# A hybrid decoder layer on one NeuronCore: the first half written as a table of steps, k and q0 projected first, the softmax scaling moved from GpSimd to VectorE

## The chip, the cores and the metric

The kernel runs on one core of one Trainium2 chip. A core has a matrix engine (TensorE, PE in the rows), three further engines that compute (VectorE, ScalarE, GpSimd: DVE, ACT, POOL in the rows) and SyncE (SP), which issues most DMA transfers. Each engine takes its own instructions in order and waits for the others on semaphores. The metric is the time of one launch in microseconds.

## The reference

One decoder layer in fp32 on a sequence of 1024 tokens with 1024 channels:

```python
h = rms_norm(x, norm_mix_g)
q, k, v, u, gate = split(h @ w_in)          # 512, 128, 128, 512, 512 columns
q, k = rms_norm per head of 64              # 8 query heads, 2 kv heads
a = sliding_window_gqa(q, k, v, sinks, rel_bias)   # window 128, blocks of 128 queries
c = u * sigmoid(gate)
c = silu(layer_norm(causal_depthwise_conv31(c)))
mix = concat(rms_norm(a), rms_norm(c))
x = x + mix @ w_out
h = rms_norm(x, norm_mlp_g)
x = x + square(relu(h @ w_up)) @ w_down     # hidden 4096
```

In the attention each block of 128 queries sees its own and the previous block of keys, with a bias from a table and one sink value per head in the softmax.

## The kernel before

Activations lie with channels on the partitions. A product in fp32 is made of three matmuls on operands split into a high and a low part: hi·hi, hi·lo, lo·hi (`mm3k`, lines 194 to 200). A weight tile is 128 output channels by 1024 (8 blocks `kc`); with two halves h of 512 tokens it makes 48 matmuls of 128x512. These are called dense here. The low part of a weight tile (`wlo`, L168) is made on VectorE, the high part (`whi`, L167) on ScalarE, some tiles ahead of use.

The layer's first part has these stages:

- `start` loads x, makes its squares' sum for the RMS norm and multiplies the first two weight tiles while x arrives.
- The combined projection: pairs u0 to u3 (a u tile and its gate tile; `ug`, then `hglu` and `conv`), q0 to q3, k and v (`qkv`). `qk_stats` makes the norms of q and k heads, with a power on GpSimd (L507).
- 16 attention units (j, bp), head pair j and block pair bp. `attn_a`: QK on PE into two banks `sc` (L567), scaling on ScalarE (L574), bias and maximum on VectorE in one reduce (L575). `attn_b`: the maximum's arithmetic, four exps on ScalarE (L591), the sum `den` and its reciprocal on VectorE, and the scaling of the probabilities on GpSimd (L596, L597, L599). `attn_c`: transposes on PE (L616), their evacuation `pT`, PV on PE (L625), evacuation into Q.
- Conv: layer norm `ln` (token Z), `silu` (S), `norm_conv` (C); attention's norm `norm_attn` (N). C and N write the halves of `mix`, split into high (ScalarE, L658) and low (GpSimd, L659).
- Output projection in two parts: `out_conv(h)` with the conv's half of mix, `out(h)` with attention's half; `out` also sums squares of the result (L744 on GpSimd). `x1_norm` (X) and `gen_h0`, `gen_h1` (G) make the normalised, split input of the MLP.
- The MLP: ten first tiles of up (`up_first`), then `up` and `down`, which form sums of blocks so that fewer products are needed.

What comes in which order is set by a string of tokens: `d` is one step of the dense generator chain, `u` one unit (its `attn_a`, with `attn_b` of two units earlier and `attn_c` of four units earlier), letters with a half start a slow generator, `+n` advances it. Everything but the dense work is emitted at a raised priority; a scheduler then orders each engine's instructions from the emission, the priorities and the readiness that it expects.

```python
ORDER = "u1,u2,u3,k,q0,v,q1,q2,q3"
SCHED = "d d d d d d d d d d d d Z0 Z1 S0 S1 C0 C1 d +2 d +2 ..."
```

Of the kernel before, what the change touches and what calls it, by code (L numbers as in the profile page):

```python
# [12 lines left out]
F32 = mybir.dt.float32  # L13
# [20 lines left out]
NU1 = 2  # L34
# [3 lines left out]
BOOST0 = 3000  # L38
BOOST = 200
LAG_B = 2  # L40
LAG_C = 4
UNITS = "00,01,10,11,20,21,30,31,02,03,12,13,22,23,32,33"
ORDER = "u1,u2,u3,k,q0,v,q1,q2,q3"
SCHED = "d d d d d d d d d d d d Z0 Z1 S0 S1 C0 C1 d +2 d +2 d +2 d +2 d +4 d +4 u d +1 u d +1 u d +1 u d +1 u d +1 u d +1 u d d u d u d d u d u d u d N0 +9 u d u d u d u d u d u d u d u d X0 N1 G0 +2 d +2 d +2 d +2 d +2 d +2 d +2 d +2 d d d d d d d d d d d X1 G1 +1 d +3 d +2 d +2 d +2 d +2 d +2 d +2 d +2"
# [22 lines left out]

class Builder:
    def __init__(self, ctx, tc, io):
        self.tc = tc  # L70
        self.nc = tc.nc
        self.io = io
# [52 lines left out]

    def run(self, gen):
        for _ in gen:
            self.flush()

    def flush(self):  # L130
        while self.bg_step(1):
            pass

    def slow_step(self, n):
        for _ in range(n):
            while self.slow:
                with self.tc.high_priority(self.slow[0][1]) if self.slow[0][1] else ExitStack():
                    self.pin_all = self.slow[0][2]
                    more = next(self.slow[0][0], None) is not None
                    self.pin_all = False  # L140
                    if more:
                        break
                self.slow.pop(0)

    def bg_step(self, n):
        for _ in range(n):
            if not self.bg:
                return False
            with self.tc.high_priority(BOOST):
                if next(self.bg[0], None) is None:  # L150
                    self.bg.pop(0)
        return True
# [41 lines left out]
    def mm3k(self, ps, w, x, kc, first, last):  # L194
        nc = self.nc
        ws = slice(kc * P, (kc + 1) * P)
        xh, xl = x
        nc.tensor.matmul(ps, w[0][:, ws], xh, start=first, stop=False)  # L198
        nc.tensor.matmul(ps, w[0][:, ws], xl, start=False, stop=False)  # L199
        nc.tensor.matmul(ps, w[1][:, ws], xh, start=False, stop=last)  # L200
# [14 lines left out]
    def build(self):  # L215
# [29 lines left out]
        for _ in range(4):  # L245
            nc.tensor.matmul(ps[:, :256], zero[:, :P], zero[:, :256], start=True, stop=True)
# [15 lines left out]
        nc.scalar.activation(warm, self.mhalf[:, 0:1], AF.Sigmoid)  # L262
        self.conv_load(0)
        self.start()
        self.mix = {}
        self.bg = []
        self.slow = []
        self.rq_done = set()
        self.qkv_begin()
# [19 lines left out]
        for tok in SCHED.split():  # L289
# [8 lines left out]
            elif tok[-1] == "d":  # L298
                for _ in range(int(tok[:-1] or 1)):
                    next(dense)  # L300
                    self.flush()
# [10 lines left out]
        for _ in dense:  # L312
            pass
# [843 lines left out]
```

## Time and profile before

| | |
|---|---|
| time, median of 3 runs | 1023.99 us (1022.13 to 1025.24) |
| the profiled execution's own time | 1022.33 us |
| its span (first to last instruction) | 1020.4 us |
| mean granted clock of PE | 0.983 |
| PE busy | 996.5 us (98%) |
| VectorE busy | 668.7 us (66%) |
| ScalarE busy | 493.2 us (48%) |
| GpSimd busy | 104.1 us (10%) |

The profile is one execution. PE is busy for nearly the whole span, but matmuls in the first part sometimes run at a lower granted clock, which counts as busy as well. Averages over the span mix the stages, so the rows further below are cut into stretches. The ScalarE order holds seven loads of an activation table, the GpSimd order 86 rows.

### The profile page before, as it was taken

The numbers are of one execution on the slowest core, as the hardware profiler recorded it, in microseconds if no ns is written. First come the engines' busy times: TensorE is split into PE (matmuls) and PEld (weight loads), VectorE is DVE, ScalarE is ACT, GpSimd is POOL, SyncE is SP. The second block draws the span as 40 slices with busy tenths as digits, with TensorE's granted clock in tenths as the row PEclk, the third lists the DMA queues.
The fourth block names the chain that finished last, engine by engine and source line by source line (L and its number), as shares of the span: only waits on it lengthen the run. The fifth ranks groups of instructions, "written<-read, shape, count | busy, mean of one in ns | idle before, by whom it ended". The sixth has DMA issues, their size and how long they took to land.

```text
span 1020.4 us, 14870 instructions
## 1 busy us (share of the span) xinstructions
PE 996.5 (98%) x5560; PEld 806.2 (79%) x5560; DVE 668.7 (66%) x1150; ACT 493.2 (48%) x946; POOL 104.1 (10%) x82
## 2 busy tenths in 40 slices
PE   8999999899979989999999999999999999999998
PEld 7888887677657768778888888888888888888886
DVE  7456535266667484598777786777774777747763
ACT  7332325766757445475444544536454343443442
POOL 1000012255143322200000000000000000000000
PEclk9999999799979999999999999999999999999999
DMA  9123300002200234446556655667875532346451
GB/s 354 60 70 136 125 32 11 11 12 93 73 11 32 90 122 139 145 171 215 194 194 220 237 185 205 239 225 255 285 264 188 183 130 99 103 135 216 165 165 42
DMA packets 67464, 148.72 MB, mean 146 GB/s; under 512 B 7776, under 2 KB 8032, under 8 KB 66880
## 3 DMA queue, kind: packets, MB, share of 16 engines
q1 hardware_dynamic: 67248, 147.75, 42.3%
q8 instruction: 44, 0.72, 0.3%
q14 instruction: 28, 0.23, 0.1%
q10 hardware_dynamic: 144, 0.02, 0.0%
HBM read 106.98 MB, written 38.80 MB: 143 GB/s over the span
## 4 chain that ended last, share of the span: by engine, by line
PE 89%; DVE 5%; ACT 3%; issue 1%; DMA 1%; POOL 0%; DVEq 0%; SPq 0%; ACTq 0%
PE mm L198 7%; PE mm L199 7%; PE mm L200 7%; PE sc L837 4%; PE sc L839 4%; PE sc L838 4%; PE tr L839 3%; PE tr L837 3%; PE tr L838 3%; PE sc L567 3%; PE mm L839 3%; PE mm L837 3%; PE mm L838 3%; PE mm L1057 3%; PE mm L1058 3%; PE mm L1059 3%
## 5 line engine op out<-in xcount | busy, mean ns | idle before, releaser
L763 ACT CAST wb<-wd 128x512 fp32r<-128x512 f32 x80 | 49.8, 622 | 111.3 <-DVE wd L1025 41.7
L764 DVE TENSOR_TENSOR wb<-wd,wb 128x512 fp32r<-128x512 f32 x80 | 55.3, 691 | 69.9 <-ACT wb L763 69.9
L167 ACT CAST whi<-raw 128x512 fp32r<-128x512 f32 (+1 forms) x54 | 42.9, 795 | 77.2 <-PE mm L199 55.4
L198 PE MATMUL mm<-xh,whi 128*128 128x512 f32 x192 | 77.8, 405 | 0.0
L199 PE MATMUL mm<-xl,whi 128*128 128x512 f32 x192 | 77.2, 402 | 0.0
L200 PE MATMUL mm<-xh,wlo 128*128 128x512 f32 x192 | 77.2, 402 | 0.0
L764 DVE TENSOR_TENSOR wb<-hb,wb 128x512 fp32r<-128x512 f32 x112 | 76.8, 685 | 0.0
L837 PE MATMUL sc<-op,wb 128*128 128x512 f32 x192 | 74.7, 389 | 0.0
L838 PE MATMUL sc<-op,wb 128*128 128x512 f32 x192 | 74.7, 389 | 0.0
L839 PE MATMUL sc<-op,wb 128*128 128x512 f32 x192 | 74.7, 389 | 0.0
L763 ACT CAST wb<-hb 128x512 fp32r<-128x512 f32 x112 | 69.0, 616 | 0.3 <-PE sc L839 0.3
L168 DVE TENSOR_TENSOR wlo<-raw,whi 128x512 fp32r<-128x512 f32 (+1 forms) x54 | 52.8, 979 | 16.8 <-ACT whi L167 11.5
L763 ACT CAST wb<-raw 128x512 fp32r<-128x512 f32 x46 | 27.7, 621 | 65.4 <-DVE raw L891 33.0
L198 PE MATMUL mm<-mix,whi 128*128 128x512 f32 x128 | 52.6, 412 | 3.3 <-ACT x1g L763 2.9
L200 PE MATMUL mm<-mix,wlo 128*128 128x512 f32 x128 | 52.5, 410 | 0.3 <-DVE wlo L168 0.3
L199 PE MATMUL mm<-mix,whi 128*128 128x512 f32 x128 | 52.4, 410 | 0.0
L1058 PE MATMUL mm<-wb,wb 128*128 128x512 f32 x128 | 49.8, 389 | 0.0
L1058 PE MATMUL sc<-wb,wb 128*128 128x512 f32 x128 | 49.8, 389 | 0.0
L837 PE MATMUL tr<-op,wb 128*128 128x512 f32 x128 | 49.8, 389 | 0.0
L838 PE MATMUL tr<-op,wb 128*128 128x512 f32 x128 | 49.8, 389 | 0.0
L1059 PE MATMUL mm<-wb,wb 128*128 128x512 f32 x128 | 49.6, 389 | 0.0
L1059 PE MATMUL sc<-wb,wb 128*128 128x512 f32 x128 | 49.6, 389 | 0.0
(270 smaller groups left out, 2532.9 us busy)
## 6 DMA issues: line engine op xcount, KB each, us to landing
hb<-hid SPq DMA_DIRECT2D x112, 256.0 KB, 2.9
wd<-w_down SPq DMA_DIRECT2D x80, 256.0 KB, 4.4
raw<-w_up SPq DMA_DIRECT2D x27, 512.0 KB, 3.5
hid<-h SPq DMA_DIRECT2D x48, 256.0 KB, 2.9
pa<-pa SPq DMA_DIRECT2D x20, 512.0 KB, 4.5
raw<-w_out SPq DMA_DIRECT2D x32, 256.0 KB, 2.6
hid<-pa SPq DMA_DIRECT2D x32, 256.0 KB, 2.9
hid<-tu SPq DMA_DIRECT2D x32, 256.0 KB, 3.3
```

Source lines behind the costliest of these rows:

```text
L167: self.pin(nc.scalar.copy(hi, raw))
L168: self.pin(eng.tensor_tensor(lo, raw, hi.bitcast(F32), ALU.subtract))
L198: nc.tensor.matmul(ps, w[0][:, ws], xh, start=first, stop=False)
L199: nc.tensor.matmul(ps, w[0][:, ws], xl, start=False, stop=False)
L200: nc.tensor.matmul(ps, w[1][:, ws], xh, start=False, stop=last)
L763: self.pin(self.nc.scalar.copy(hi, src))
L764: self.pin(eng.tensor_tensor(lo, src, hi.bitcast(F32), ALU.subtract))
L837: nc.tensor.matmul(ps, wh[:, c], xh, start=first and k == 0, stop=False, skip_group_check=True)
L838: nc.tensor.matmul(ps, wh[:, c], xl, start=False, stop=False, skip_group_check=True)
L839: nc.tensor.matmul(ps, wl[:, c], xh, start=False, stop=last and k == len(xs) - 1, skip_group_check=True)
L1058: nc.tensor.matmul(pss[m], wh[:, c], bl, start=False, stop=False, skip_group_check=True)
L1059: nc.tensor.matmul(pss[m], wl[:, c], bh, start=False, stop=f == NP - 1, skip_group_check=True)
```

## The change

The token string, the priorities and the background generators are gone. A table `SIDE` says which pieces of side work are emitted at which of the numbered steps; a step is 12 dense matmuls, since `mm3` now yields in its middle. Units A (QK and softmax), T (transposes) and V (PV) are three pieces. `start` multiplies k and q0 instead of u0 and its gate. The dense order is u0 to u3, v, q1 to q3, both out_conv, both out, the ten up_first. Units of j = 0 stand beside u1 to u3, the other twelve at steps 43 to 57. `Pinned` sends each PE instruction through `put`, which keeps program order where `on` is True; the code sets `on` to False in both places where it sets it.

```diff
-ORDER = "u1,u2,u3,k,q0,v,q1,q2,q3"
-SCHED = "d d d d d d d d d d d d Z0 Z1 S0 S1 C0 C1 d +2 ..."
+ORDER = "u0,u1,u2,u3,v,q1,q2,q3"
+U_EARLY, U_LATE = (9, 13, 17, 21), ("10", "11", "20", "21", "30", "31", "12", "13", "22", "23", "32", "33")
+LATE = (43, 44, 47, 48, 51, 51, 52, 53, 54, 55, 56, 57)
+SIDE = {2: "rs", 3: "st4 st0", 5: "rb st0", 6: "st4", 7: "st4", 12: "c0", 20: "c1", 28: "c2",
+        36: "c3", 37: "vt", 38: "vt Z0", 40: "Z1", 41: "st1", 42: "st1 S0 S0", 43: "S0 S0", 44: "S1 S1", 45: "S1 S1",
+        46: "C0 st2", 47: "C0 C0 st2", 49: "st3 C1", 50: "st3", 51: "C1 C1",
...
+for n, at in enumerate(U_EARLY):
+    SIDE[at] = SIDE.get(at, "") + f" A0{n}"
+    SIDE[at + 4] = SIDE.get(at + 4, "") + f" T0{n}"
+    SIDE[39 + n] = SIDE.get(39 + n, "") + f" V0{n}"
...
+class Pinned:
+    def __init__(self, tc):
+        self.tc, self.on = tc, False
+
+    def put(self, ins):
+        if self.on:
+            self.tc.keep_in_program_order(ins)
...
     def mm3(self, ps, w, xs):
         for kc, x in enumerate(xs):
+            if kc == 4:
+                yield True
             self.mm3k(ps, w, x, kc, kc == 0, kc == len(xs) - 1)
...
+        k = 0
+        while True:
+            for a in SIDE.get(k, "").split():
+                if a[0] == "A":
+                    st[a[1:]] = self.attn_a(int(a[1]), int(a[2]))
+                    self.attn_b(st[a[1:]])
...
+            k += 1
+            if not next(dense, False):
+                break
...
-            ps = [self.psum("x"), self.psum("o")]
+            ps = [self.psum(t) for t in (("x", "o"), ("sc", "sc"))[jh]]
...
-        if bp == 0:
-            nc.gpsimd.tensor_tensor(s[:, 0:2, P:], s[:, 0:2, P:], rd[:, 0:2].unsqueeze(2).broadcast_to([P, 2, P]), ALU.mult)
-            nc.gpsimd.tensor_tensor(s[:, 2:4, :], s[:, 2:4, :], rd[:, 2:4].unsqueeze(2).broadcast_to([P, 2, 256]), ALU.mult)
-        else:
-            nc.gpsimd.tensor_tensor(s, s, rd.unsqueeze(2).broadcast_to([P, 4, 256]), ALU.mult)
+        for i in range(4):
+            lo = P if bp == 0 and i < 2 else 0
+            nc.vector.tensor_scalar(s[:, i, lo:], s[:, i, lo:], rd[:, i:i + 1], None, ALU.mult)
...
-            self.evac(EVAC.get(u["i"], "aaa")[c], pT[:, c, i0 * P:], ps[:, i0 * P:])
+            self.evac("a" if u["j"] == 0 else "v", pT[:, c, i0 * P:], ps[:, i0 * P:])
...
-            nc.gpsimd.tensor_tensor(mt[:, 1, :], s, mt[:, 0, :].bitcast(F32), ALU.subtract)
+            nc.vector.tensor_tensor(mt[:, 1, :], s, mt[:, 0, :].bitcast(F32), ALU.subtract)
...
+        rs = self.small("rs1", 4)
+        self.rsqrt(rs, mv3[:, :, 1], 1.0, 4)
...
-                nc.gpsimd.tensor_tensor(acc, acc, sq, ALU.add)
+                nc.vector.tensor_tensor(acc, acc, sq, ALU.add)
```

`ln` makes the powers of its four tiles in one instruction. Tiles of the output X for h = 1 and slots of the operand tiles `op` and `wd` lie in other pools. The order of the weights' loads follows the dense order.

How the change moves instructions is seen in the orders that the scheduler built. First GpSimd, between two of the norms' powers, from the middle of the first part: before, the softmax scalings of a unit (s by rd) and the low halves of mix stand between them.

```order
L507 TENSOR_TENSOR qst_2035<-qst_2035,mhalf 128x16
L599 TENSOR_TENSOR s_1982<-s_1982,rd_2147 128x1024
L596 TENSOR_TENSOR s_2085<-s_2085,rd_2261 128x2x128
L597 TENSOR_TENSOR s_2085<-s_2085,rd_2261 128x512
L210 TENSOR_TENSOR rc_2140<-rs_2141,mhalf 128x4
L599 TENSOR_TENSOR s_2181<-s_2181,rd_2356 128x1024
L659 TENSOR_TENSOR mix_2245<-y_498,mix_2245 128x512
```

In the change the whole of GpSimd's work after the start is powers: r for x, qst for q and k, rs for the layer norm, rc for the norms of mix and x1.

```order
L505 TENSOR_TENSOR qst_410<-qst_410,mhalf 128x16
L207 TENSOR_TENSOR rs_211_1838<-rs_1839,mhalf 128x4
L207 TENSOR_TENSOR rs_227_1917<-rs_1918,mhalf 128x4
L505 TENSOR_TENSOR qst_1965<-qst_1965,mhalf 128x16
L505 TENSOR_TENSOR qst_2201<-qst_2201,mhalf 128x16
L207 TENSOR_TENSOR rc_2234<-rs_2235,mhalf 128x4
L505 TENSOR_TENSOR qst_2394<-qst_2394,mhalf 128x16
L207 TENSOR_TENSOR rc_2481<-rs_2482,mhalf 128x4
```

So 86 rows became 30, and every 128x512 or larger operation has left GpSimd.

Second VectorE, in one of the late units, beside the output projection. Before, its queue has reduces (ISA is the custom reduce, with a read of its result), small operations of the maximum and of den, an evacuation, and a residual add and a low half for the weights:

```order
L575 ISA s_2561,mx_2562<-s_2561,bias_304 128x256
L575 ISA mx_2562 128x1
L727 TENSOR_TENSOR X_2670<-mm_2657,xr_2655 128x512
L593 TENSOR_TENSOR den_2602<-den_2602,es_2601 128x4
L603 COPY pT_2615<-tr_2616 128x256
L594 RECIPROCAL rd_2603<-den_2602 128x4
L168 TENSOR_TENSOR wlo_2728<-raw_2577,whi_2727 128x512
```

In the change the same piece of a unit reads:

```order
L588 TENSOR_TENSOR den_2697<-den_2697,es_2696 128x4
L581 SCALAR_TENSOR_TENSOR nm_2775<-mx_2760,nsink 128x4
L589 RECIPROCAL rd_2698<-den_2697 128x4
L582 TENSOR_TENSOR es_2776<-nm_2775,nsink 128x4
L720 TENSOR_TENSOR Xp_3093<-mm_3137,xr_3135 128x512
L592 TENSOR_SCALAR s_2679<-s_2679,rd_2698 128x256 x4
L596 COPY pT_2815<-tr_2816 128x512
L163 TENSOR_TENSOR wlo_3186<-raw_3072,whi_3185 128x512
L596 COPY pT_2815<-tr_2822 128x512
```

Four scalings and both evacuations of each late unit have come into VectorE's queue, ahead of the low half for a weight tile of the output projection.

Third ScalarE, at the layer norm's silu (L696 and L693; y from the transposed z). Before, the silus of the first half stand together, and a table load comes where the function changes:

```order
L592 ACT_TABLE_LOAD
L592 ACTIVATE es_1883<-es_1883 128x4
L574 ACTIVATE s_1815<-sc_1817,rq 128x256 x2
L574 ACTIVATE s_1815<-sc_1818,rq 128x256 x2
L696 ACT_TABLE_LOAD
L696 ACTIVATE y_498<-tr_1730,pv 128x512
L696 ACTIVATE y_787<-tr_1736,pv 128x512
```

In the change, rows 140 to 156 of ScalarE's order:

```order
L693 ACTIVATE y_1472<-tr_2030,pv 128x512
L693 ACTIVATE y_1748<-tr_2036,pv 128x512
L586 ACT_TABLE_LOAD
L586 ACTIVATE s_2042,den_2060<-s_2042,nm_2058 128x128 x2
L586 ACTIVATE s_2042,den_2060<-s_2042,nm_2058 128x256 x2
L587 ACTIVATE es_2059<-es_2059 128x4
L162 CAST whi_2137<-raw_1752 128x512
L484 COPY Q_307<-mm_2017 128x512
L693 ACT_TABLE_LOAD
L693 ACTIVATE y_767<-tr_2090,pv 128x512
L586 ACT_TABLE_LOAD
```

Units and silus alternate there; the whole order has eleven table loads where the one before has seven.

## Rows read from the trace of the kernel before

**Rows 1.** Windows: stretch, length; busy (count) PE, PEld, DVE, ACT, POOL; PEclk, DMA, GB/s

```profile
50.00:150.00 100.00, 100.00 (x1397) 81.37 (x1396) 52.19 (x58) 30.86 (x48) 2.90 (x1) 1.00 0.27 90
150.00:231.00 81.00, 75.46 (x393) 60.07 (x392) 42.31 (x126) 52.22 (x126) 30.19 (x25) 0.93 0.04 14
231.00:412.00 181.00, 172.00 (x909) 129.53 (x908) 111.77 (x243) 103.42 (x255) 62.18 (x41) 0.94 0.25 82
460.60:1016.20 555.60, 555.37 (x2448) 459.11 (x2447) 393.26 (x627) 248.59 (x434) 0.00 (x0) 1.00 0.55 188
200.00:350.00 150.00, 144.39 (x803) 105.62 (x803) 91.56 (x242) 96.91 (x273) 62.17 (x41) 0.92 0.15 46
290.00:305.00 15.00, 13.63 (x51) 9.51 (x52) 7.99 (x17) 6.93 (x20) 7.99 (x6) 0.61 0.01 1
365.00:385.00 20.00, 16.61 (x64) 12.79 (x64) 19.19 (x26) 8.82 (x14) 5.15 (x4) 0.91 0.40 132
```

**Rows 2.** Matmul lines: duration ns min/median/max, first and last start (us), form

```profile
L198 PE MATMUL mm<-xh,whi x192: 387/389/774, 28.5 to 226.1; 128*128 128x512 f32 x192
L198 PE MATMUL mm<-mix,whi x128: 387/390/628, 230.2 to 411.0; 128*128 128x512 f32 x128
L837 PE MATMUL mm<-x1g,wb x48: 389/389/389, 460.6 to 691.2; 128*128 128x512 f32 x48
```

**Rows 3.** Timeline 221.5 to 225: start us, us, engine, line, operation

```profile
221.87 2.10 DVE L575 CUSTOM_DVE_ANT_0 s<-s,bias 128x256 f32<-128x256 f32 x1
224.16 0.42 DVE L575 CUSTOM_DVE_ANT_0 s<-s,bias 128x256 f32<-128x256 f32 x1
...
221.80 1.89 POOL L599 TENSOR_TENSOR s<-s,rd 128x1024 f32<-128x1024 f32 x1 [1.25 <-DVE rd L594]
```

**Rows 4.** Lines by source: duration ns min/median/max, first and last start (us)

```profile
L575 DVE CUSTOM_DVE_ANT_0 s<-s,bias x64: 260/423/2109, 169.9 to 325.6; 128x256 f32<-128x256 f32 x56, 128x128 f32<-128x128 f32 x8
...
L168 DVE TENSOR_TENSOR wlo<-raw,whi x54: 659/693/2095, 20.6 to 454.2; 128x512 fp32r<-128x512 f32 x32, 128x1024 fp32r<-128x1024 f32 x22
...
L507 POOL TENSOR_TENSOR qst<-qst,mhalf x5: 2899/2904/3391, 130.3 to 243.4; 128x16 f32<-128x16 f32 x5
...
L210 POOL TENSOR_TENSOR rc<-rs,mhalf x6: 1007/1014/1969, 196.6 to 418.4; 128x4 f32<-128x4 f32 x6
```

**Rows 5.** VectorE's groups: busy us, mean ns; idle before, releaser

```profile
L575 DVE CUSTOM_DVE_ANT_0 s<-s,bias 128x256 f32<-128x256 f32 x56 | 37.8, 706 | 6.0 <-ACT s L574 5.8
L648 DVE SCALAR_TENSOR_TENSOR y<-y,pv,sc 128x512 f32<-128x512 f32 x8 | 5.4, 743 | 4.4 <-PE sc L393 4.4
L603 DVE COPY pT<-tr 128x512 f32<-128x512 f32 x5 | 3.4, 686 | 2.4 <-PE tr L616 2.4
L593 DVE TENSOR_TENSOR den<-den,es 128x4 f32<-128x4 f32 x16 | 2.6, 161 | 11.2 <-ACT es L592 9.4 <-ACT s L591 1.9
L603 DVE COPY Q<-o 128x256 f32<-128x256 f32 x6 | 2.5, 424 | 5.1 <-PE o L625 5.1
L518 DVE COPY kc<-rk 128x512 f32<-128x512 f32 x2 | 0.8, 424 | 0.0
```

**Rows 6.** PE's groups from 50 to 150 us

```profile
L198 PE MATMUL mm<-xh,whi 128*128 128x512 f32 x103 | 40.9, 397 | 0.0
```

**Rows 7.** Chain of work: start us, us, what

```profile
245.55 1.02 PE tr L616 x8
...
320.33 1.06 PE sc L567 x6
321.39 0.81 PE o L625 x12
```

**Rows 8.** ScalarE's groups: busy us, mean ns; idle before, releaser

```profile
L696 ACT ACTIVATE y<-tr,pv 128x512 f32<-128x512 f32 x8 | 5.8, 774 | 0.1
L696 ACT ACT_TABLE_LOAD x3 | 3.8, 1283 | 0.1
L637 ACT ACTIVATE sq<-y 128x512 f32<-128x512 f32 x6 | 3.8, 640 | 1.4 <-PE tr L501 1.4
```

More of the change, by code (lines that the diff above doesn't have):

```diff
@@ L124, in chain @@
                 yield True
[L126 to L152, printed above, removed]
     def load_w(self, src):
@@ L245, in build @@
         for _ in range(4):
-            nc.tensor.matmul(ps[:, :256], zero[:, :P], zero[:, :256], start=True, stop=True)
+            self.pe.matmul(ps[:, :256], zero[:, :P], zero[:, :256], start=True, stop=True)
         self.ones = cp.tile([P, 1], F32, tag="ones", name="ones")
@@ L262, in build @@
         nc.scalar.activation(warm, self.mhalf[:, 0:1], AF.Sigmoid)
+        self.mix = {}
+        self.gens = {}
+        self.hg = [None] * NCT
+        self.start()
         self.conv_load(0)
[L264 to L269, printed above, removed]
         self.X = {}
@@ L280, in build @@
-        dense.append(self.out(1))
-        dense += [self.up_first(i) for i in FIRST[NU1:]]
-        dense.append(self.up())
-        dense.append(self.down())
+        dense = [make[n]() for n in ORDER.split(",")]
+        dense += [self.out_conv(0, range(KC)), self.out_conv(1, range(KC)), self.out(0), self.out(1)]
+        dense += [self.up_first(i) for i in FIRST]
         dense = self.chain(dense)
-        units = [(int(a[0]), int(a[1])) for a in UNITS.split(",")]
+        side = {"Z": self.ln, "S": self.silu, "C": self.norm_conv, "N": self.norm_attn, "X": self.x1_norm,
+                "G": lambda h: self.gen_h0(h) if h == 0 else self.gen_h1(h)}
@@ L311, in build @@
-        assert i >= n + LAG_C
-        for _ in dense:
-            pass
+        k = 0
[4 more added lines that the diff above has]
+                    self.attn_b(st[a[1:]])
+                elif a[0] == "T":
+                    self.attn_t(st[a[1:]])
+                elif a[0] == "V":
+                    self.attn_v(st[a[1:]])
+                else:
+                    if a not in self.gens:
+                        self.gens[a] = side[a[0]](int(a[1]))
+                    self.pin_all = a[0] == "G"
+                    assert next(self.gens[a])
+                    self.pin_all = False
+            k += 1
+            if not next(dense, False):
+                break
@@ L641, in norm_half @@
         for i in range(4):
-            nc.tensor.matmul(ps[:, i:i + 1], acc[:, i * P:(i + 1) * P], self.ones[:, 0:1], start=True, stop=True)
+            self.pe.matmul(ps[:, i:i + 1], acc[:, i * P:(i + 1) * P], self.ones[:, 0:1], start=True, stop=True)
         rc = self.small("rc", 4)
@@ L724, in out_conv @@
             ps = self.psum("mm")
-            self.mm3(ps, w, [self.mix[kc, h] for kc in range(4, KC)])
+            yield from self.mm3(ps, w, [self.mix[kc, h] for kc in range(4, KC)])
             X = self.X[m, h] = self.x_tile(m, h)
@@ L735, in out @@
             ps = self.psum("mm")
-            self.mm3(ps, w, [self.mix[kc, h] for kc in range(4)])
+            yield from self.mm3(ps, w, [self.mix[kc, h] for kc in range(4)])
             X = self.X[m, h]
@@ L753, in x1_norm @@
         for i in range(4):
-            nc.tensor.matmul(ps[:, i:i + 1], acc[:, i * P:(i + 1) * P], self.ones[:, 0:1], start=True, stop=True)
+            self.pe.matmul(ps[:, i:i + 1], acc[:, i * P:(i + 1) * P], self.ones[:, 0:1], start=True, stop=True)
         rc = self.small("rc", 4)
```

242 lines of the change are left out of this document (111 added, 131 removed), and 3 rows, old and new, of the table SIDE.

## The prediction, written before the changed kernel ran

> **What bounds the kernel now.** I read the windows first. From 460.6 us to the end the PE is busy for 555.37 of 555.60 us with 2448 matmuls, all 128x512: 0.227 us each [rows 1]. The change leaves that stretch nearly as it is, so it is a constant. The stretch 50 to 150 is as full, 100.00 of 100. Between 150 and 412 there are holes: 75.46 of 81 and 172.00 of 181, at a granted clock of 0.93 and 0.94 [rows 1]. So the slack is in 150 to 412: 14.5 us of idle PE and some slow clock. No engine is full there: from 231 to 412 VectorE has 111.77 us of work, ScalarE 103.42, GpSimd 62.18 [rows 1]. The PE waits for chains that pass through several engines.
>
> Next I read the first and last starts of the matmul lines. The projection's weights (xh) run from 28.5 to 226.1, the output projection (mix) from 230.2 to 411.0, and up proper starts at 460.6 [rows 2]. The time to forecast is when the changed kernel reaches that last point.
>
> Last, one place that shows why the middle is slow. A reduce of 128x256 on VectorE takes 0.42 us at 224.16, and 2.10 us at 221.87, where a GpSimd scaling ran from 221.80 for 1.89 us [rows 3]. Over all calls the median is 0.423 and the mean of the 56 large ones 0.706 [rows 4, 5]: 56 × 0.28 = 15.8 us lost. The lo halves of weights go up to 2.095 against a median of 0.693 [rows 4].
>
> **The change part by part.** I count in the order that the scheduler built, not in the table of steps: `on`, which would pin PE to program order, is never set to True, so the steps are only the order in which work is offered. The dense work is the same: 1200 matmuls of 128x512 lie between 28.5 and the start of up.
>
> *1. Start to the statistics of q1.* The start computes k and q0 instead of u0 with the same 96 matmuls, so 28.5 stays. Up to the row where PE takes q1's statistics the new order has 492 dense matmuls: 492 × 0.227 = 111.7. The stretch 50 to 150 of before holds the conv and the other small work that now stands there: its 309 dense matmuls (3 × 103 [rows 6]) make 70.1, the other 29.9. To this come three more QK (1.06 each), four more sets of transposes (1.02), three PV (0.81) [rows 7], 9.7 in all, and some 7 us for layer-norm transposes, v's transposes and sums, an estimate by the same rows. For stalls I take 2 us: the conv's second half now stands in the sc banks that QK uses, so a QK waits there for copies of yt; at four conv tiles and two copies each, at most the 0.64 of a 128x512 operation there [rows 8], that is 0 to 5. 28.5 + 111.7 + 29.9 + 16.8 + 2 = **189**. VectorE has 52.19 of 100 us to do in this stretch now [rows 1]; the four units beside u1 to u3 add about 3.8 us each by the prices of part 4, so it hides there. Loads and slots (X, op and wd tiles in other pools, the weights in another order on SP's queue) cost nothing: the DMA engines are 4% and 25% busy from 150 to 412 [rows 1]. If a slot came free late, one load of a few us would show.
>
> *2. q2 and q3.* Here ScalarE, in order, has rows 126 to 163: five table loads of 1.283, since silu and exp alternate (6.4), eight silus of 0.774 (6.2) [rows 8], and 40 others at the mean of the stretch 150 to 231, 52.22 / 126 = 0.41 (16.6) [rows 1]. Together 29.2, against 19 us for the 84 dense matmuls that PE has left of the projection, so ScalarE sets the end: 189 + 29.2, about **219**. The layer norm's batched power costs about 1.0 per half, as a 128x4 power does now [rows 4].
>
> *3. To the first output product.* A chain: four squares of 0.64 on ScalarE [rows 8], 2.6; the adds and pT copies on VectorE that the squares don't cover, 3.2; sums with ones 0.5; the power with its scaling 1.2. Then GpSimd has the power of q3's statistics, 2.9 [rows 4], and its consumer stands in VectorE's queue ahead of the multiplies. Then four multiplies of 0.743 [rows 5], 3.0, and the first subtracts between reduces, 4. In all 17.4: **236.5**. The chain is of the kind that makes the holes of before.
>
> *4. The late units.* This is the term that decides. From the first subtract to the last one of N1 (VectorE rows 230 to 430 of the new order) VectorE is given 46 operations of 128x512 with two inputs (lo halves, residual adds, subtracts, square sums) × 0.69 = 31.7; 18 pT copies of 0.686 and two of 0.42, 13.2; eight multiplies of 0.743, 5.9; 38 reduces of 0.423 and 40 reads of 0.08, 19.3; 42 small ones of 0.161, 6.8 [rows 4, 5]; and 40 new scalings. A TENSOR_SCALAR of 128x256 does not occur before. Below, it is half the SBUF copy of 128x512, 0.424 / 2 = 0.21; above, the copy of 128x256 that takes 0.424 [rows 5]. I take 0.29: the copy's 0.424 and a small operation's 0.161 give a fixed part of about 0.16 and half of the rest. 40 × 0.29 = 11.4 (8.5 to 17). The sum is 88.3 us.
>
> The reduces are priced at their median because GpSimd has only powers left. The Trainium skill, GPSIMD Engine Reference, section 1 (Specifications), says that GpSimd shares its SBUF interface with VectorE and collides with instructions that have two SBUF inputs or a two-port mode; the 2.10 us above agree. By that rule the three powers left in this stretch could each hold a scaling for its 1.0 us, 3 us more; by the rows alone nothing is added.
>
> Waits add to the 88.3. VectorE takes its queue in order: a unit's den waits for its exps (four on ScalarE), reduces behind it wait with it, and the multiplies of N0 and N1 wait for a chain. In before, dens waited 11.2 us in 16 units and reduces 6.0 [rows 5]; ten units here give about 7 + 4, and N0, N1 about 2 each: 15. 236.5 + 103.3 = **340**. That is 85% busy; from 200 to 350 VectorE was 61% busy, from 365 to 385 96% [rows 1].
>
> *5. Second part of the output projection.* 192 dense matmuls are 43.6; VectorE's 61 rows from 431 to 491 (x1's pieces, adds, lo halves) come to 64 × 0.69 = 44.2. Plus 2.5 until X0's power is back. **387**.
>
> *6. First products of up.* 240 × 0.227 = 54.5, plus 1.7 for x1's sums and 2.7 where B21's last pieces come late. Plus 3 us of half clock after the hole of part 3, as before had at 290 to 305 (granted 0.61) [rows 1]. **448.7** instead of 460.6: 11.9 us less. The evacuations that move from ScalarE to VectorE are in the sum; ScalarE, freed of them, has under 60% to do in that stretch.
>
> **The sum.** 1020.4 − 11.9 = 1008.5 of span; the profiled run has 1022.33, 1.93 outside its span, so 1010.4. The profiled run lies 1.66 under the median of 1023.99, so the forecast for a median is **1012**. A change of ±0.3% (3 us) is what can be told from none.
>
> **The rivals**, all on part 4, since its length is 88.3 over the busy share of VectorE:
> - *Even better.* VectorE keeps the 96% of 365 to 385: 92 us, another 11 less: 1001. Against it: in those 20 us only few softmax waits fell.
> - *No change.* Waits eat it: at 75% part 4 takes 118 us and the end is 1026. At 76% it is even.
> - *Slower.* VectorE becomes the bound and waits in order: reduce, exp, den, scaling and pT copy of one unit are now all in one queue behind one another, with the weights' lo halves for PE in between. At 70% it is 126, so 1035; at the 61% of 200 to 350, 145, so 1054. For it: rows 314 to 360 show dens and copies ahead of the lo half of the next weight. Against it: those 61% held GpSimd's collisions and the work was less, so VectorE had nothing to do rather than waits. It decides at 76%.
> - *The clock.* With PE only some 70% busy in part 4, the granted clock may fall to the lower of its levels (0.5, 1.2 of 2.4 GHz). PE's work there, about 72 us at full clock, becomes 103 at a mean of 0.70: only below that does PE set the end. At 0.61 for the whole stretch (290 to 305) it takes 118: 1027. TensorE: Matmul & The Clock Gate of the Trainium skill, section "HAM oscillation", describes kernels whose clock swings between the levels when PE idles between groups; 0.61 at 290 to 305, after holes, agrees. I count this with the slower case.
>
> **Chances.** Forecast (1003 to 1020.5) 0.50; even better 0.12; no change 0.13; slower 0.25, clock included. Faster is then 0.62. The range of 8 in 10 leaves out about a third of the better case and some 0.15 of the slowest: 1000 to 1036. A scaling at 0.42 would add 5 us, at 0.21 take 3 off; both lie inside.
>
> **What would show it.** Right: u0 from 28.5; q1's statistics on PE at about 189; the first matmul with mix near 236; reduces with a mean near 0.43 and a maximum under 1; TENSOR_SCALAR of 128x256 near 0.29; VectorE over 80% busy from 236 to 340; up from about 449. Wrong: GpSimd gone but reduces still long; a scaling above 0.42; VectorE under 76% in the middle with den waiting for exp; a clock under 0.7 from 236 to 340; holes ahead of q1, where I put only 2 us.

## The result and the profile after

The changed kernel takes 994.45 us (median of 4 runs, 990.88 to 994.56) against 1023.12 before on the same chip: a ratio of 0.9707, 95% interval 0.9689 to 0.9726, so 2.9% less. The forecast was 1012 with a range of 1000 to 1036: the direction came out, the size did not.

The profiled execution has a span of 989.1 us, 31.3 less. Its windows, with the columns of [rows 1], and ahead of them the one window of before that covers the same work:

```profile
28.50:460.60 432.10, 414.98 (x3009) 326.51 (x3008) 253.38 (x494) 222.32 (x487) 101.40 (x71) 0.96 0.24 78
```

```profile
28.50:429.40 400.90, 395.01 (x3011) 318.73 (x3011) 272.80 (x603) 223.22 (x483) 26.65 (x16) 0.98 0.26 86
28.50:50.00 21.50, 21.50 (x115) 18.59 (x115) 6.97 (x15) 6.15 (x11) 7.67 (x5) 0.92 0.07 26
50.00:150.00 100.00, 100.00 (x1182) 81.62 (x1182) 57.09 (x112) 49.30 (x104) 0.00 (x0) 1.00 0.26 87
150.00:189.00 39.00, 37.25 (x432) 30.39 (x431) 21.04 (x33) 12.63 (x25) 1.45 (x2) 0.96 0.14 42
189.00:219.00 30.00, 30.00 (x185) 24.17 (x183) 10.21 (x40) 21.99 (x48) 3.46 (x2) 1.00 0.03 10
219.00:235.40 16.40, 15.25 (x96) 13.43 (x95) 9.50 (x21) 9.17 (x18) 7.17 (x3) 0.69 0.05 16
235.40:325.00 89.60, 88.22 (x544) 67.35 (x543) 76.90 (x242) 59.57 (x176) 2.13 (x2) 1.00 0.27 89
235.40:370.70 135.30, 133.34 (x754) 104.01 (x753) 113.90 (x303) 83.41 (x216) 4.95 (x4) 1.00 0.27 92
429.40:984.00 554.60, 554.38 (x2444) 458.50 (x2444) 387.68 (x616) 245.47 (x429) 0.00 (x0) 1.00 0.55 187
```

The first line of each is the whole stretch from the first weights to the start of up: 432.1 us before, 400.9 now. So all of the gain lies there; up and down behind it are as full as in [rows 1] (2444 matmuls in 554.6 us). The number of PE instructions in the stretch is the same (3009, 3011). PE is idle for 17.1 us of it before and 5.9 now, 11.2 less; and its busy time falls from 415.0 to 395.0, 20.0 less for the same work. The mean granted clock is 0.98 instead of 0.96.

From the lines by source: the first and last products with mix and the first with x1g, then the reduce, the new scaling and the low halves (they answer to [rows 2] and [rows 4]):

```profile
L86 PE MATMUL mm<-mix,whi x256: 387/389/504, 235.4 to 370.1; 128*128 128x512 f32 x128
...
L86 PE MATMUL mm<-x1g,whi x160: 387/389/501, 370.7 to 429.0; 128*128 128x512 f32 x160
L86 PE MATMUL mm<-x1g,wb x144: 389/389/389, 429.4 to 660.4; 128*128 128x512 f32 x144
...
L572 DVE CUSTOM_DVE_ANT_0 s<-s,bias x64: 279/419/426, 65.6 to 306.2; 128x256 f32<-128x256 f32 x56, 128x128 f32<-128x128 f32 x8
...
L592 DVE TENSOR_SCALAR s<-s,rd x64: 277/348/354, 75.1 to 312.9; 128x256 f32<-128x256 f32 x56, 128x128 f32<-128x128 f32 x8
...
L163 DVE TENSOR_TENSOR wlo<-raw,whi x54: 673/684/1226, 20.6 to 420.6; 128x512 fp32r<-128x512 f32 x32, 128x1024 fp32r<-128x1024 f32 x22
```

The first output product comes at 235.4, up at 429.4. The reduces have a maximum of 0.426 where [rows 4] has 2.109, the low halves 1.226 (a 128x1024) where it has 2.095.

Where did 20 us of busy PE time go? I added up, for each kind of matmul in the stretch, the time from its start to the next one's start or its own end, whichever comes first. Dense matmuls fall from 292.1 to 288.1, PV from 19.3 to 16.7, transposes of s from 15.7 to 14.1, and the 128 QK matmuls from 33.1 to 22.7.

A part of this is the clock. The windows of 6 us or more in which PE was granted the lower of its two levels (0.50, that is 1.2 of 2.4 GHz), three before and one after:

```profile
192.20:202.44 10.24, 8.25 (x24) 6.29 (x24) 4.28 (x14) 4.96 (x13) 6.70 (x4) 0.50 0.08 26
287.79:294.61 6.82, 5.16 (x30) 4.74 (x31) 1.85 (x4) 1.71 (x8) 3.67 (x3) 0.50 0.00 0
298.02:308.26 10.24, 10.24 (x36) 6.77 (x37) 7.96 (x18) 5.67 (x17) 5.79 (x4) 0.50 0.01 2
...
223.60:233.84 10.24, 10.18 (x51) 9.55 (x52) 5.28 (x14) 4.48 (x9) 5.68 (x3) 0.50 0.00 0
```

With two shorter windows on each side, PE is busy at the lower level for 30.5 us before and 17.0 after. A dense matmul takes 0.43 us from start to start there and 0.24 elsewhere, so the 13.5 us less are worth about 6 of the 20 (an estimate from these numbers).

Another part is QK. PE's timeline shows how two units of the same size differ, one early and one late:

```profile
83.19 1.14 PE L86 MATMUL sc<-kh,Q 64*128 64x256 f32 x8
...
270.95 1.13 PE L86 MATMUL sc<-kh,Q 64*128 64x256 f32 x4
272.01 0.88 PE L89 MATMUL tr<-ident,s 128*128 128x128 f32 x6
272.82 1.13 PE L86 MATMUL sc<-kh,Q 64*128 64x256 f32 x4
```

At 83.19 eight matmuls of 64 rows take 1.14 us; at 270.95 and 272.82 four take 1.13 each. In the first, matmuls on the upper and on the lower 64 rows start 7 ns apart and run side by side; in the second, one half's four stand alone, because transposes of another unit lie between the halves in PE's order. Why the scheduler put them there (the halves write two banks, and they may be expected free one after the other) is argued, not shown. Counting matmuls that follow their neighbour within 50 ns, 38 of 128 ran so in the profile after and 11 before. At the full clock a matmul of such a pair costs 0.13 us and one alone 0.25 to 0.27, so the 27 more pairs make some 7 to 8 of QK's 10.4 us; some of the rest is the clock.

### The profile page after: what moved, and what is told of

Read it like the earlier page. It is cut to its first block, busy times and chain, and to the rows that moved or that the text cites. A ratio compares the mean times of both kernels' runs of the same rounds, so it can differ in the third digit from the quotient of the medians.

```text
span 989.1 us, 14838 instructions
## 1 busy us (share of the span) xinstructions
PE 976.7 (99%) x5560; PEld 798.0 (81%) x5560; DVE 683.5 (69%) x1250; ACT 490.9 (50%) x938; POOL 29.3 (3%) x25
## 4 chain that ended last, share of the span: by engine, by line
PE 91%; DVE 4%; ACT 2%; DMA 1%; issue 1%; SPq 0%; DVEq 0%; ACTq 0%
PE mm L86 37%; PE sc L86 26%; PE tr L86 17%; PE o L86 5%; PE x L86 4%; PE tr L89 1%; DMA xraw<-xT 1%; DVE Q L642 1%; DMA wd<-w_down 1%; ACT wb L756 0%; SPq L135 0%; DVE wlo L163 0%; DVE X L1068 0%; ACT y L693 0%; DVE wb L757 0%
## 5 line engine op out<-in xcount | busy, mean ns | idle before, releaser
L86 PE MATMUL sc<-op,wb 128*128 128x512 f32 x576 | 136.6, 389 | 0.0
L86 PEld LDWEIGHTS sc<-op,wb 128*128 128x128 f32 x576 | 108.1, 188 | 22.4
L86 PE MATMUL tr<-op,wb 128*128 128x512 f32 x384 | 91.3, 389 | 0.0
L86 PE MATMUL mm<-mix,whi 128*128 128x512 f32 x256 | 82.9, 401 | 1.8 <-DVE mix L653 0.8
L86 PEld LDWEIGHTS mm<-wb,wb 128*128 128x128 f32 x384 | 72.0, 188 | 15.4 <-ACT wb L756 0.5
L86 PEld LDWEIGHTS sc<-wb,wb 128*128 128x128 f32 x384 | 72.1, 188 | 15.0
L86 PEld LDWEIGHTS tr<-op,wb 128*128 128x128 f32 x384 | 72.1, 188 | 14.9
L86 PE MATMUL tr<-wb,wb 128*128 128x512 f32 x288 | 78.4, 389 | 0.1
L86 PEld LDWEIGHTS tr<-wb,wb 128*128 128x128 f32 x288 | 54.0, 188 | 11.7 <-ACT wb L756 0.5
L86 PEld LDWEIGHTS mm<-mix,whi 128*128 128x128 f32 x256 | 46.6, 188 | 14.1 <-issue 3.4
```

Of the source, the lines that this page charges most:

```text
L86: self.put(self.tc.nc.tensor.matmul(*a, **k))
```

## The experiments

Each was timed in five rounds against the kernel before on the same chip. Ratios are to that kernel; the changed kernel itself stands at 0.9707.

| run | what it does | median us | ratio (95% interval) |
|---|---|---|---|
| e1_qk_g_outer | QK written half by half | 995.98 | 0.9709 (0.9684 to 0.9735) |
| e2_scale_gpsimd | scaling back on GpSimd | 1000.44 | 0.9759 (0.9736 to 0.9782) |
| e3_scale_twice | scaling twice on VectorE | 1007.57 | 0.9832 (0.9808 to 0.9857) |
| e4_before_dve | before, GpSimd only powers | 1012.26 | 0.9879 (0.9857 to 0.9901) |
| e5_no_early | no units beside u1 to u3 | 1033.42 | 1.0089 (1.0065 to 1.0113) |
| e6_pt_scalar | pT copies on ScalarE | 1001.88 | 0.9767 (0.9740 to 0.9793) |
| e7_pt_split | one pT copy on each | 995.51 | 0.9719 (0.9696 to 0.9742) |
| e8_pinned | PE in the written order | 1011.74 | 0.9865 (0.9836 to 0.9894) |
| e9_qk_order | QK alone in the written order | 1002.01 | 0.9775 (0.9751 to 0.9799) |
| e10_silu_first | first late units at step 46 | 1009.57 | 0.9861 (0.9840 to 0.9881) |
| e11_no_early_pt_dve | e5, pT copies on VectorE | 1028.49 | 1.0047 (1.0029 to 1.0064) |
| e12_less_pe | 64 dense matmuls left out | 990.68 | 0.9677 (0.9653 to 0.9701) |
| e13_no_scale | scaling left out | 995.97 | 0.9714 (0.9692 to 0.9735) |
| e14_no_wlo | low halves of 16 tiles left out | 1001.29 | 0.9766 (0.9741 to 0.9791) |
| e15_units_earlier | first late units at step 42 | 999.64 | 0.9749 (0.9717 to 0.9781) |
| e16_again | the changed kernel | 996.57 | 0.9724 (0.9705 to 0.9743) |

The last one is the control: a repeat beside e13 to e15 came out 0.2% away, with 0.9724. Differences of up to 0.3% between the experiments are read as none. A profile is one execution with a time of its own; it was 1011.03 us for e3, 1005.68 for e8, 1004.18 for e9 and 995.93 for e14.

**First: PE's own time or VectorE's queue.** Two theories stood after the result. Theory 1: PE sets the end, and holes closed and QK halves run side by side. Theory 2, the prediction's: VectorE's queue, freed of GpSimd's collisions, sets the end of the middle.

```diff
# e1_qk_g_outer
-        for b2 in range(2):
-            ...
-            for g in range(2):
+        for g in range(2):
+            ...
+            for b2 in range(2):
```

> The changed kernel with one edit: the eight QK matmuls of a unit are written with the row half g in the outer loop, so that neighbours on PE use the same half of the rows. Theory 1 (PE's own time: neighbours of different row halves run at once, and PE sets the end of the middle): the 38 overlapped pairs of the changed kernel go, a unit costs about 2.12 us instead of 1.07, so 38 x 0.26 = 10 us more, about 1004 us. Theory 2 (VectorE's queue, freed of GpSimd's collisions, sets the end of the middle): the PE order of eight small matmuls is hidden, 994 within 2 us.

Measured 995.98, no change. But the edit did not do what it was meant to: 36 of 128 QK matmuls still ran beside a neighbour. PE's timeline of e1, the unit that answers to 83.19 above:

```profile
85.05 1.14 PE L86 MATMUL sc<-kh,Q 64*128 64x256 f32 x8
```

Four matmuls of one half now stand ahead of four of the other in program order, in the order that the scheduler built too, and all eight take 1.14 us. So the order within a unit does not decide on the overlap, and the run says nothing for or against theory 1.

```diff
# e2_scale_gpsimd (bp > 0)
-            nc.vector.tensor_scalar(s[:, i, lo:], s[:, i, lo:], rd[:, i:i + 1], None, ALU.mult)
+            nc.gpsimd.tensor_tensor(s, s, rd.unsqueeze(2).broadcast_to([P, 4, 256]), ALU.mult)
```

> The changed kernel with the softmax scaling back on GpSimd, as one to two instructions per unit. Theory 1: VectorE loses the scalings (64 x 0.28 = 18 us) and gets collisions in the reduces back (mean 0.7 instead of 0.42, some 16 us); it has slack, so the time stays within 4 us of 994. Theory 2: collisions and the longer chain of a unit (1.98 instead of 1.13) lengthen the late units by 10 us or more: 1004 to 1012.

Measured 1000.44, 0.4 to 0.5% more than the changed kernel (against its repeat or its first timing): between the two. The collisions are back, as the reduce's line by source shows (maximum 2.117, median as before):

```profile
L572 DVE CUSTOM_DVE_ANT_0 s<-s,bias x64: 285/420/2117, 70.1 to 316.9; 128x256 f32<-128x256 f32 x56, 128x128 f32<-128x128 f32 x8
```

```diff
# e3_scale_twice
             nc.vector.tensor_scalar(s[:, i, lo:], s[:, i, lo:], rd[:, i:i + 1], None, ALU.mult)
+        for i in range(4):
+            lo = P if bp == 0 and i < 2 else 0
+            nc.vector.tensor_scalar(s[:, i, lo:], s[:, i, lo:], self.ones[:, 0:1], None, ALU.mult)
```

> The changed kernel with each softmax scaling followed by a second pass over the same data that multiplies by ones: 64 more VectorE instructions of 0.28 us, 18 us in all, 40 of them (11 us) in the late units. Theory 1: VectorE has about 13 of 90 us idle in the late stretch, so 0 to 4 us more. Theory 2: VectorE sets the end there, 11 us more: about 1005.

Measured 1007.57, 11 to 13 us more (against the repeat or the first timing), as theory 2 has it. The stretch from the first product with mix to the last grew from 135 to 147 us:

```profile
240.90:388.00 147.10, 142.22 (x753) 109.02 (x752) 121.17 (x338) 83.12 (x211) 5.25 (x4) 0.96 0.26 85
320.00:360.00 40.00, 35.27 (x217) 28.40 (x216) 30.02 (x70) 16.13 (x36) 2.62 (x2) 0.87 0.12 40
```

The loss sits behind the units, from 320 to 360: the units now end after the conv half of the output projection has run out, PE has 4.7 us of holes, and its clock falls to 0.87.

```diff
# e4_before_dve: the kernel before, softmax scaling as above, and
-            nc.gpsimd.tensor_tensor(mt[:, 1, :], s, mt[:, 0, :].bitcast(F32), ALU.subtract)
+            nc.vector.tensor_tensor(mt[:, 1, :], s, mt[:, 0, :].bitcast(F32), ALU.subtract)
-                nc.gpsimd.tensor_tensor(acc, acc, sq, ALU.add)
+                nc.vector.tensor_tensor(acc, acc, sq, ALU.add)
```

> The kernel before with one part of the change alone: softmax scaling as four instructions on VectorE, the low half of mix and the squares' sum on VectorE, so that GpSimd has powers only; steps, orders and evacuations stay. Theory 2: most of the gain comes with it, 1023 down to about 1005. Theory 1: reduces fall to 0.42, but the holes of PE (17 us) and the QK pairs (11) stay much as they were: 1017 to 1023.

Measured 1012.26, 1.2% less than before. The engine moves alone bring some 12 of the 29 us, more than theory 1 and less than theory 2 said. The reduces have a maximum of 0.428 there.

**Second: what of the order counts.**

```diff
# e5_no_early: A at 40 to 43, T three and V five steps later
-for n, at in enumerate(U_EARLY):
+for n, at in enumerate((40, 41, 42, 43)):
```

> The changed kernel with the four units of j = 0 at steps 40 to 43 instead of beside u1 to u3; all else stays. If VectorE's queue sets the length of the late stage, four more units there (four reduces 1.4, four scalings 1.1, small ones 0.4 each by starting distance; their pT copies stay on ScalarE) give 4 x 2.9 / 0.855 = 13.6 us more, about 1008. If the early place only matters for PE's filling (PE was full from 50 to 150 before as well), under 4 us.

Measured 1033.42: 37 to 39 us more than the changed kernel, and slower than before. This was far outside what either theory gave. Most of the loss, 32 us, lies not in the late stage but in the stretch ahead of the first output product, which comes at 267 instead of 235. Windows, and what PE waited for from 200 to 270 (engine, tile, line; us in total, times, longest):

```profile
206.00:268.00 62.00, 46.41 (x231) 36.33 (x229) 28.11 (x104) 46.39 (x107) 7.17 (x3) 0.61 0.02 5
```

```profile
PE tr L89 <- ACT y L693: 12.2, 4, 4.1
PE sc L86 <- ACT s L571: 3.0, 2, 1.9
```

PE has 15.6 us of holes and a mean clock of 0.61 there. The chain of waits in that stretch runs through ScalarE, back and forth between exp (L586) and silu (L693):

```profile
213.96 1.28 ACT L586
215.25 2.08 ACT s L586 x8
217.44 1.28 ACT L693
218.74 0.79 ACT y L693
...
```

Each pair costs two table loads of 1.28 us: eight loads stand between 200 and 241 us, where the changed kernel has five, though the kernel as a whole has ten and the changed one eleven. ScalarE is busy for 46.4 of the 62 us and VectorE for 28.1, so the early units matter because they take exps away from where silu and statistics are due, and not because of VectorE. Holes are only one half of the price. Its window from 28.5 to the start of up:

```profile
28.50:470.20 441.70, 417.73 (x3012) 332.92 (x3011) 276.20 (x603) 223.16 (x483) 26.73 (x16) 0.93 0.24 78
```

PE is idle for 24.0 us instead of 5.9 and busy for 417.7 instead of 395.0 with the same number of instructions, at a mean clock of 0.93 instead of 0.98: 18 us of holes, and 23 of slower matmuls.

```diff
# e6_pt_scalar
-            self.evac("a" if u["j"] == 0 else "v", pT[:, c, i0 * P:], ps[:, i0 * P:])
+            self.evac("a", pT[:, c, i0 * P:], ps[:, i0 * P:])
# e7_pt_split
+            self.evac("a" if u["j"] == 0 or c == 0 else "v", pT[:, c, i0 * P:], ps[:, i0 * P:])
```

> The changed kernel with all pT evacuations on ScalarE. Takes 24 copies of 0.60 us (starting distance) from VectorE, 20 of them in the late stage: 12 us / 0.855 = 14 us less if VectorE alone sets its length, about 981. ScalarE, 59.6 of 89.6 us busy there, gets 10 to 12 us more. If a unit's chain through the engines sets the length instead, the copies are as long on ScalarE and wait behind exps: 994 within 4 us.

> The changed kernel with the first of a unit's two pT copies on ScalarE and the second on VectorE. VectorE alone: 6 us / 0.855 = 7 us less, 987. Chain of a unit: the two copies go side by side, 0.6 us less per unit at most, 990 to 994.

Measured 1001.88 and 995.51: 0.4 to 0.6% more, and no change. Taking 12 us from VectorE in the late stage shortened nothing, so VectorE's queue alone does not set its length (e6 gives the copies to ScalarE, so it doesn't settle it by itself). This is against theory 2.

```diff
# e8_pinned
-        self.tc, self.on = tc, False
+        self.tc, self.on = tc, True
```

> The changed kernel with the attribute on at True until up starts, so that PE keeps the order in which the table of steps emits. The work on each engine is the same. If VectorE sets the late stage and its queue is the same, 994 within 5 us. If PE lives from filling holes by the scheduler's own order, PE waits in the written order: over 1000.

Measured 1011.74. In the written order PE is idle for 25.2 of 415.7 us:

```profile
28.50:444.20 415.70, 390.47 (x3019) 317.45 (x3019) 275.09 (x603) 224.85 (x485) 26.25 (x16) 0.98 0.26 83
```

although 56 of the QK matmuls ran beside a neighbour. With 0.9865 the written order has a little under half of the gain over before; the rest comes from the order that the scheduler makes of the steps.

**Third: PE in the late stage, and the stretch ahead of it.**

```diff
# e9_qk_order
-                self.pe.matmul(psv[g][:, b2, 256 - W:], ..., start=True, stop=True)
+                self.tc.keep_in_program_order(self.nc.tensor.matmul(psv[g][:, b2, 256 - W:], ..., start=True, stop=True))
# e10_silu_first
-LATE = (43, 44, 47, 48, 51, 51, 52, 53, 54, 55, 56, 57)
+LATE = (46, 46, 47, 48, 51, 51, 52, 53, 54, 55, 56, 57)
```

> The changed kernel with the QK matmuls alone kept in program order, so that the two row halves of a unit alternate and a unit starts when both banks are free. If PE's own time sets the late stage, QK falls from 22.7 to about 18 us and the time by 4 to 5, about 990. If waiting for the second bank costs as much as the overlap gives, 994 within 3 us; more if VectorE then runs dry.

Measured 1002.01. 52 QK matmuls ran beside a neighbour and QK took 20.7 us, 2 less; but in the profile, at 1004.18 us the slowest of the five, PE's idle time rose from 5.9 to 10.3 us (414.2 less 403.9 busy) and its mean clock fell to 0.95. So more is lost elsewhere than the overlap gives. That it is lost by waiting for the second bank does not show: PE's waits in the late stage there name no copy out of those banks, and how much the clock took by itself is open.

> The changed kernel with the first two late units at step 46 instead of 43 and 44, so that the silus stand closer together: nine activation table loads in place of eleven. If ScalarE's queue sets the time of the first output product, 2 x 1.28 us less there, and the two units' softmax (about 9 us of ScalarE) comes behind it: first mix 5 to 10 us earlier, and the late stage has two units more, 2 x 2.9 to 2 x 4.1 / 0.855, 7 to 10 us. 990 to 998 in all. If ScalarE does not set it, the first mix stays at 235 and the time goes to about 1003.

Measured 1009.57, worse than either case. Two table loads fewer did not help: the first product with mix came at 249. PE waited 5.3 us in one piece for a square of q (L487). The chain of waits shows what held it: ScalarE's square came after the add of the squares' sum (L632), which stood in VectorE's queue behind a unit's scalings and a low half:

```profile
PE tr L86 <- ACT sq L487: 5.3, 1, 5.3
```

```profile
235.21 0.87 DVE s L592 x3
236.08 0.60 DVE wlo L163
236.68 0.09 DVE rq L509
236.76 0.61 DVE nacc L632
237.40 0.61 ACT sq L487
238.05 1.88 PE tr L86 x8
```

So what shows there is VectorE's and ScalarE's order around the first output product, and not the count of table loads.

> The kernel without early units (the four units of j = 0 at steps 40 to 43), with their pT copies on VectorE instead of ScalarE. There the first mix came at 267 us and ScalarE was 92% busy from 200 to 240. If ScalarE's queue is what put it off, 8 copies of 0.5 less: the first mix 3 to 5 us earlier, 1029 to 1031 us. If VectorE's queue or the bare length of a unit's chain did, it stays at 267 or comes later: 1033 to 1037.

The edit is that of e5 with `self.evac("v", ...)`. Measured 1028.49, the first product with mix at 263.0 instead of 267.4: the 3 to 5 us that ScalarE's queue gives.

```diff
# e12_less_pe: in mm3k, for out_conv alone
-        self.pe.matmul(ps, w[0][:, ws], xl, start=False, stop=False)
+        if lo:
+            self.pe.matmul(ps, w[0][:, ws], xl, start=False, stop=False)
```

> The changed kernel without the products with the low half of mix in the conv half of the output projection (64 matmuls of 128x512, 14.5 us of PE, are left out; the low halves are still made). VectorE, ScalarE and GpSimd have the same work. If PE sets the length of the late stage, the time falls by 12 to 15 us to 980 to 982. If VectorE's queue sets it, as the prediction has it, by 0 to 4: 990 to 994.

Measured 990.68: a ratio of 0.9677 against 0.9707 and, for the repeat, 0.9724, so 3 to 5 us less, at the edge of what can be told from none. Its profile shows the stage itself 7 us shorter, 128.3 from the first product with mix to the last instead of 135.3. Of 14.5 us of PE about half came through at most. PE now waits for the units at their end, and VectorE is 94% busy:

```profile
240.90:369.20 128.30, 121.52 (x689) 93.08 (x688) 112.69 (x302) 82.25 (x214) 4.96 (x4) 1.00 0.31 95
300.00:320.00 20.00, 15.09 (x144) 11.71 (x145) 18.82 (x66) 15.13 (x49) 1.01 (x1) 1.00 0.00 1
```

```profile
PE tr L89 <- DVE s L593: 2.1, 1, 2.1
PE o L86 <- ACT mix L653: 1.3, 1, 1.3
```

**Fourth: what sets the late stage.** Open by then: work added to VectorE lengthened the stage, work moved off it did not shorten it. Two runs took work off VectorE and gave it to nobody.

```diff
# e13_no_scale
-            nc.vector.tensor_scalar(s[:, i, lo:], s[:, i, lo:], rd[:, i:i + 1], None, ALU.mult)
# e14_no_wlo: in split_w, for the conv part of w_out
+        if eng is None:
+            self.pin(nc.scalar.copy(hi, raw))
+            return hi, hi
```

> The changed kernel without the softmax scaling: the probabilities stay undivided (that part of the computation is left out). VectorE loses 64 instructions of 0.28 us, 11.3 us of them in the late stage, and each unit's chain gets 1.1 us shorter. If VectorE's queue sets the late stage at 85% busy, 11 to 13 us less, 981 to 983. If PE's own time does (98% busy there), 0 to 3 us less.

> The changed kernel without the low halves of the conv part of the output weights: the high half takes their place in the same matmuls (that part of the computation is left out). VectorE loses 16 x 0.60 = 9.6 us in the late stage, PE and the units' chains keep theirs. If VectorE's queue sets the stage, 9 to 11 us less, 983 to 985. If the chain of a unit sets it (exp, den, scaling, transposes, copies), 0 to 4 less; if PE does, 0 to 2.

> The changed kernel itself on the same chip as the three others: 994 within 2 us, first output product between 235 and 241 us by the clock that PE is granted at the start.

> The changed kernel with the first two late units one step earlier, 42 and 43 instead of 43 and 44. Putting them two to three steps later cost 15 us; if that was the chain ahead of the first output product, earlier by one step gains 0 to 4: 990 to 994. If the built order hardly depends on one step, 994 within 2.

Measured 995.97, 1001.29 and, for the repeat, 996.57: no gain from either, and e14 is 0.4% slower (two of its six times lie at 996, the profiled one among them, the others at 1001 to 1003; why is open). The windows from the first product with mix to the last, for the repeat, e13 and e14:

```profile
240.40:375.80 135.40, 133.44 (x753) 104.21 (x752) 112.00 (x299) 82.40 (x212) 4.95 (x4) 0.99 0.29 90
```

```profile
237.80:372.90 135.10, 134.48 (x752) 104.14 (x752) 105.07 (x262) 83.27 (x215) 5.07 (x4) 1.00 0.29 91
```

```profile
241.10:375.30 134.20, 132.38 (x746) 103.28 (x745) 105.83 (x287) 81.07 (x211) 5.28 (x4) 1.00 0.28 87
```

135.4, 135.1 and 134.2 us, with PE busy for all but 0.6 to 2.0 us. VectorE's busy time falls from 112.0 to 105.1 and 105.8, and nothing follows. In e13 the last exps start 64 us after the first product with mix, in the changed kernel 75; the stage is as long. So in the late stage PE's work sets the length, and the units run beside it: their last exp starts at 310.0, 5 us ahead of the last add of out_conv at 314.7 (315.5 and 320.2 in the repeat). That fits e3, where the last exp starts at 327.0 and the last add is at 318.3, so the units stick out; and e12, where PE is shorter and the units show.

e15, one step earlier for two units, gave 999.64 with runs from 994.36 to 1005.03: nothing gained.

## Why the prediction was half right

**Parts 1 to 3 held.** q1's statistics stand on PE at 189.8 (forecast 189). The next statistics stand on PE at 219.6 (219), after a wait of 0.5 us for ScalarE's silus, the last of which ends at 220.2. The first product with mix comes at 235.4 (236.5), though PE ran at the lower clock for 10 us ahead of it. In part 2 the number held better than its reason: PE is full from 189 to 219 (30.00 of 30), since beside the 84 dense matmuls, 20.3 us, it has 9 us of transposes, PV, QK and statistics that the part did not count. So PE and ScalarE came out nearly level there by luck; e5 and e11 show that ScalarE's queue sets this place once more is put into it. For the conv in the sc banks one hole stands, 1.75 us at 167.2 ahead of a conv matmul; what it waited for the profile does not name.

**Part 4 failed,** and in two ways. It stood at 103.3 us; from 235.4 to the end of the last row counted (324.7) it took 89.3. (The prediction calls that end the last subtract of N1; the operations that it counts, eight multiplies among them, end with N0's subtracts and the add behind them, and N1's come at 338.5 to 341.5.) That is 14 of the 19 us by which up came earlier than forecast, 429.4 for 448.7; parts 5 and 6 have 4.

The first way is the size of VectorE's work. The step "46 operations × 0.69, 18 pT copies of 0.686, 38 reduces of 0.423 and 40 reads of 0.08 …" made 88.3 us from record lengths. VectorE's records overlap. Its timeline at 300 us:

```profile
300.18 0.42 DVE L572 CUSTOM_DVE_ANT_0 s<-s,bias 128x256 f32<-128x256 f32 x1
300.52 0.08 DVE L572 DVE_READ_ACCUMULATOR2_ANT mx<- 128x1 f32 x1
300.52 0.42 DVE L572 CUSTOM_DVE_ANT_0 s<-s,bias 128x256 f32<-128x256 f32 x1
300.87 0.08 DVE L572 DVE_READ_ACCUMULATOR2_ANT mx<- 128x1 f32 x1
300.96 0.66 DVE L720 TENSOR_TENSOR X<-mm,xr 128x512 f32<-128x512 f32 x1
301.54 0.68 DVE L163 TENSOR_TENSOR wlo<-raw,whi 128x512 fp32r<-128x512 f32 x1
302.13 0.41 DVE L572 CUSTOM_DVE_ANT_0 s<-s,bias 128x256 f32<-128x256 f32 x1
```

A reduce of 0.42 is followed after 0.34, an add of 0.66 after 0.58, a low half of 0.68 after 0.59: each record reaches some 0.08 into the next. The 241 records from 235.4 to 325.0 add up to 93.6 us, and the window 235.4 to 325 has the engine busy for 76.9. The share that I forecast, 85%, was 76.9 / 89.6 = 86%, but by luck: it was to come from VectorE's waits, and it came from a stage length that PE set. That records overlap was to be seen before: in the timeline that [rows 3] come from, a reduce of 0.28 at 223.90 is followed at 224.12.

```profile
223.90 0.28 DVE L575 CUSTOM_DVE_ANT_0 s<-s,bias 128x128 f32<-128x128 f32 x1
224.12 0.08 DVE L575 DVE_READ_ACCUMULATOR2_ANT mx<- 128x1 f32 x1
```

The price of the scaling was inside its bounds: four take 1.13 us, 0.28 each, and one alone 0.348.

The second way is the cause. The step took VectorE's queue as what sets the length, with PE's work of about 72 us lying under it; e13 and e14 show PE. PE was busy for 88.2 of 89.6 us there. Added up from start to start, 205 dense matmuls took 50.5 us (0.246 each instead of 0.227), QK 15.0, PV 10.4, transposes 8.5, sums and broadcasts 3.8. The 72 us are about what the 192 dense matmuls of out_conv (43.6) and ten units at the prices of [rows 7] (2.89 each) make, and those prices were misread: its rows hold six of a unit's eight QK matmuls and twelve of its sixteen for PV. Over all 16 units of before, QK, transposes and PV took 4.3 us each. A sum for PE would have been: from the first product with mix to up, 192 + 192 + 240 dense matmuls × 0.227 = 141.6, ten units of about 4 us, and some 6 for sums: 188, against a measured 194.0 (235.4 to 429.4) with 3 us of holes in it.

Three slips in the sums are too small to matter: 189 + 29.2 is 218 and not 219, 40 × 0.29 is 11.6 and not 11.4, and part 5 names 61 rows and prices 64.

**Parts 5 and 6** took 104.7 us instead of 108.7: the 3 us of half clock did not come (1.00 from 235.4 on; the 0.69 stands ahead, from 219 to 235.4), nor the full waits.

**The rivals.** "Even better" came nearest with its time (1001), for the wrong reason, VectorE at 96%. "Slower" and "the clock" named ends that did not come; but e3 and e5 show how near they were: 18 us more on VectorE cost 11 to 13, and the units in another place 37 to 39. Collisions with GpSimd were priced rightly in direction: e4 gives 12 us for the engine moves alone, e2 takes 4 to 5 back. The Trainium skill, GPSIMD Engine Reference, section 1 (Specifications), has GpSimd sharing its SBUF interface with VectorE; the traces agree, with a maximum of 2.117 us for the reduce with the scaling on GpSimd and 0.426 without. Whether the powers which remain could hold a scaling was not tried: the longest TENSOR_SCALAR is 0.354, but no scaling ran beside a power in the profile. Three reduces that did, at 240.3 to 241.4 us, took 0.41 to 0.42 each as elsewhere; and at 381.5 it was the power that took longer, 1.95 us instead of 1.01, beside a low half of 1.23.

What stays open: how much of the gain is QK's overlap. QK as a whole has 10.4 of the 20 us of busy time, the clock included, but no run changed the overlap alone: e1 did not change it, and e8 and e9 raised it along with holes. The clock, too, was changed by no run alone.

## What to carry to other kernels

Before an engine's queue is called the bound, make the sum for PE too, over all the work that may be let into the stage, and take what is larger; two queues of nearly equal length show little or no gain when one is relieved and nearly the full loss when one is loaded. Make an engine's sum from start to start of its records, or scale it by busy time over summed lengths. Taking the four units away from u1 to u3, where the engines had room, cost 37 to 39 us, more than the engine moves gave (12), and it showed in a stage ahead of the one that I had thought tight.

## What the runs showed of the hardware

- Matmuls on 64 rows each ran side by side when they used different halves of the rows, and that also when four of one half stood ahead of four of the other in the program (e1: eight in 1.14 us, four alone in 1.13).
- VectorE's back-to-back instructions start 0.07 to 0.09 us before the end of the record ahead of them (the timeline at 300 us).
- At the lower level of PE's clock a dense matmul took 0.43 us from start to start, and 0.24 elsewhere.
- The changed kernel's own runs lie at 990.88 once and 994.35 to 994.56 three times. In the profiled one (990.88) PE's clock is 0.92 from 28.5 to 50, in the repeat's profile 0.80, and the first product with mix comes 5 us later there; what decides on it was not tried.
